# RWKV's key grams, token transpositions and bonuses handed over one piece with every step of the inverse, from the first step on

## The chip, the cores and the metric

The kernel runs on one core of one Trainium2 chip. The metric is the device time of one execution in microseconds (us), as the median of several runs. All matrix work is TensorE's (PE), which multiplies into PSUM banks; VectorE (DVE), ScalarE (ACT) and GpSimd (POOL) move, scale and add; transfers are issued on queues of SP and POOL.

## The reference

A two-layer decoder trunk makes one step for a prompt of 256 tokens and for 8 single sample tokens, 264 columns in all, with a width of 1024, in float32. The part that matters here is the mixer of the even layer, eight heads of stick-breaking attention beside eight heads of RWKV-7:

```python
def rwkv7_recurrence(r, w, k, v, kk, a, s0):
    def step(s, inp):
        r_t, w_t, k_t, v_t, kk_t, a_t = inp
        sa = jnp.einsum('bhij,bhj->bhi', s, kk_t)
        s = (s * w_t[:, :, None, :] - sa[..., None] * (kk_t * a_t)[:, :, None, :]
             + v_t[..., None] * k_t[:, :, None, :])
        return s, jnp.einsum('bhij,bhj->bhi', s, r_t)
...
    y, wkv_final = rwkv7_recurrence(rf, heads(decay), kf, vf, kk, heads(iclr), wkv0.astype(f32))
...
    bonus = jnp.sum(rf * kf * prm['r_k'][i].astype(f32), axis=-1, keepdims=True) * vf
    o_rwkv = ((yn + bonus.reshape(bsz, t, D_RWKV)) * gate).astype(h.dtype)
    out = jnp.concatenate([o_sb, o_rwkv], axis=-1) @ prm['w_out_even'][i]
```

The samples attend to 256 cached keys and values each, gathered from a paged pool.

## The kernel before

Each dense product is done in blocks of 128x128 weights: a weight block is split into a high and a low half (`wh` on ACT, L199; `wl` on DVE, L200), and three matmuls (L297 to L299) use them. The trunk is feed-forward, mixer, feed-forward for each of two layers. The change lies in the even layer's mixer, `_even` (L643), which takes the stretch from about 280 to 417 us.

RWKV's recurrence runs in four chunks of 64 tokens. Before the chain over the chunks (`rwkv_chain`) can start, three things must be there:

- the inverse of a triangular matrix for each chunk and head (`rwkv_inverse`). Its first four steps are the grams of B (L910, into PSUM banks "rk", masked by DVE at L911 into GB). Then come levels 1 to 5, two steps each: `pP` (L935: X times the masked gram `ss`, which DVE makes at L942; ACT copies the result into `st`, L950), and `pX` (L935), after which DVE subtracts it from X (L958) and transposes X into XT (L965). That is 14 steps, and each step waits for the last.
- the pieces of `rwkv_tokens` (L858 on): four grams of K (`GK`, L910 and L911), the transpositions of B and of K to tokens (`tok`, L891, with ACT's copies into BT and KT, L898, two pieces each), four bonuses (`pbn`, L877, and `bon`, L878, which need the values `vr_t`), and the transposition of the values (VT, two pieces): 14 pieces. The K grams, the bonuses and the first half of each transposition use the one PSUM buffer of bank group "sa"; the second half of a transposition uses group "at", with two.
- the input projection's blocks of the values (`pi`, then `pb` on ACT L592, `df` on POOL L595 and L596, `vr_t` on DVE L603). These and the prompt's attention (`z`, `att`, `pcs`, `pov`) come from the generator `other_half`, called `side`.

Two more generators run beside these. `samples` holds the samples' attention: queries are transposed (`pq`, L1166), copied (`qs` on ACT, L1168), written to device memory and spread over partitions (`qd`, `qb`, on POOL's queue, L1170 and L1178), keys are gathered (`kp`, POOL's queue, L1180), multiplied (DVE, L1189) and reduced (DVE, L1190). Later, value pages `vp` are gathered (L1215) and multiplied (`pso`, L1228, in bank "sa"), and DVE masks and reduces the result (L1234, L1236). `states` does the samples' recurrence.

The loop at L685 hands pieces to a scheduler in program order, and that order sets priorities; the scheduler then fixes the order of every engine's queue. With each step of the inverse go two pieces of `side`, and from the fourth step on pieces of `tokens` and `samples` too:

```python
            if i >= 3:
                for _ in range(1 + (i > 8)):
                    next(tokens, None)
                for _ in range((i > 3) + i % 2):
                    next(samples, None)
```

So `tokens` gets one piece at each of steps 3 to 8 and two at each of steps 9 to 13, which is 16 turns; at a turn before stage 2 (the values' projection issued) a bonus that is next takes no piece. What is left is run after the loop, before the chain.

Of the kernel before, what the change touches and what calls it, by code (L numbers as in the profile page):

```python
# [220 lines left out]
class Trunk:  # L221
# [383 lines left out]
    def _even(self, ctx, ln_in, ln_out):  # L605
# [75 lines left out]
        tokens = self.rwkv_tokens(bone)  # L681
# [3 lines left out]
        for i, _ in enumerate(self.rwkv_inverse()):  # L685
            for _ in range(2):
                next(side)
            if i >= 3:
                for _ in range(1 + (i > 8)):
                    next(tokens, None)  # L690
                for _ in range((i > 3) + i % 2):
                    next(samples, None)
        while self.stage < 2:
# [1272 lines left out]
```

## Time and profile before

| what | value |
|---|---|
| runs shown | 1161.09, 1162.82, 1162.86 us; median 1162.82 us |
| profiled execution | 1161.34 us |
| its span | 1159.6 us, mean granted TensorE clock 0.983 |
| PE busy | 1098.3 us (95%) |
| DVE busy | 870.8 us (75%) |
| ACT busy | 592.2 us (51%) |
| POOL busy | 170.4 us (15%) |

Times in the rows are microseconds from the start of the profiled span. A bracket behind a row tells how long the engine had been idle ahead of it and what it then got. "PEclk" is the share of TensorE's full speed that was granted.

### The profile page before, as it was taken

The numbers are of one execution on the slowest core, as the hardware profiler recorded it, in microseconds if no ns is written. First come the engines' busy times: TensorE is split into PE (matmuls) and PEld (weight loads), VectorE is DVE, ScalarE is ACT, GpSimd is POOL, SyncE is SP. The second block draws the span as 40 slices with busy tenths as digits, with TensorE's granted clock in tenths as the row PEclk, the third lists the DMA queues.
The fourth block names the chain that finished last, engine by engine and source line by source line (L and its number), as shares of the span: only waits on it lengthen the run. The fifth ranks groups of instructions, "written<-read, shape, count | busy, mean of one in ns | idle before, by whom it ended". The sixth has DMA issues, their size and how long they took to land. (4 is left out here: it accounts for less than half of the span.)

```text
span 1159.6 us, 25702 instructions
## 1 busy us (share of the span) xinstructions
PE 1098.3 (95%) x10391; PEld 1050.4 (91%) x10391; DVE 870.8 (75%) x1726; ACT 592.2 (51%) x1043; POOL 170.4 (15%) x284
## 2 busy tenths in 40 slices
PE   7999999998889899999999999999969999999996
PEld 7999999987777679999999999999958899999995
DVE  4999855878887969888776888666579689555564
ACT  5544554686344556644454654453363366444442
POOL 0000000355545322011100112000020001000000
PEclk9999999999989999999999999999979999999998
DMA  7654656633455434566775567655474354655551
GB/s 254 231 169 157 211 181 217 199 111 127 155 154 171 150 105 146 169 222 231 256 216 181 163 204 220 204 182 180 146 231 129 117 167 137 210 181 183 181 174 46
DMA packets 66119, 204.91 MB, mean 177 GB/s; under 512 B 13464, under 2 KB 16616, under 8 KB 65744
## 3 DMA queue, kind: packets, MB, share of 16 engines
q1 hardware_dynamic: 56400, 174.09, 47.6%
q0 software_dynamic: 6560, 23.27, 6.1%
q10 hardware_dynamic: 3040, 5.92, 1.6%
q8 instruction: 81, 1.33, 0.5%
q14 instruction: 38, 0.31, 0.1%
HBM read 192.22 MB, written 10.86 MB: 175 GB/s over the span
## 5 line engine op out<-in xcount | busy, mean ns | idle before, releaser
L200 DVE TENSOR_TENSOR wl<-raw,wh 128x1024 fp32r<-128x1024 f32 (+2 forms) x317 | 388.1, 1225 | 183.8 <-ACT wh L199 182.6
L199 ACT CAST wh<-raw 128x1024 fp32r<-128x1024 f32 (+2 forms) x317 | 329.9, 1041 | 320.2 <-issue 103.6
L297 PE MATMUL pd<-hh,wh 128*128 128x264 f32 x704 | 200.8, 285 | 0.0
L299 PE MATMUL pd<-hh,wl 128*128 128x264 f32 x704 | 200.7, 285 | 0.0
L298 PE MATMUL pd<-hl,wh 128*128 128x264 f32 x704 | 199.1, 283 | 0.0
L297 PE MATMUL pg<-xh,wh 128*128 128x264 f32 x648 | 185.0, 285 | 5.6 <-DVE fixc L469 4.0
L299 PE MATMUL pg<-xh,wl 128*128 128x264 f32 x648 | 184.6, 285 | 1.4 <-DVE wl L200 1.3
L298 PE MATMUL pg<-xl,wh 128*128 128x264 f32 x648 | 184.0, 284 | 0.0
L299 PE MATMUL pu<-xh,wl 128*128 128x264 f32 x608 | 172.9, 284 | 1.8 <-DVE wl L200 1.7
L297 PE MATMUL pu<-xh,wh 128*128 128x264 f32 x608 | 172.7, 284 | 0.0
L298 PE MATMUL pu<-xl,wh 128*128 128x264 f32 x608 | 172.3, 283 | 0.0
L297 PEld LDWEIGHTS pd<-hh,wh 128*128 128x128 f32 x704 | 132.4, 188 | 0.6
L299 PEld LDWEIGHTS pd<-hh,wl 128*128 128x128 f32 x704 | 132.6, 188 | 0.2
L298 PEld LDWEIGHTS pd<-hl,wh 128*128 128x128 f32 x704 | 132.4, 188 | 0.0
L297 PEld LDWEIGHTS pg<-xh,wh 128*128 128x128 f32 x648 | 122.6, 189 | 6.5 <-ACT xh L453 4.4
L299 PEld LDWEIGHTS pg<-xh,wl 128*128 128x128 f32 x648 | 122.1, 188 | 2.5 <-DVE wl L200 2.4
L298 PEld LDWEIGHTS pg<-xl,wh 128*128 128x128 f32 x648 | 122.6, 189 | 0.0
L299 PEld LDWEIGHTS pu<-xh,wl 128*128 128x128 f32 x608 | 114.1, 188 | 2.9 <-DVE wl L200 2.9
L297 PEld LDWEIGHTS pu<-xh,wh 128*128 128x128 f32 x608 | 114.8, 189 | 0.0
L298 PEld LDWEIGHTS pu<-xl,wh 128*128 128x128 f32 x608 | 114.8, 189 | 0.0
L500 ACT CAST hh<-h 128x264 fp32r<-128x264 f32 x79 | 32.2, 409 | 55.1 <-DVE h L499 55.1
L297 PE MATMUL raw<-rh,wh 128*128 128x266 f32 x192 | 55.9, 291 | 0.1
(548 smaller groups left out, 2153.6 us busy)
## 6 DMA issues: line engine op xcount, KB each, us to landing
raw<-in_w SPq DMA_DIRECT2D x308, 512.0 KB, 3.7
raw<-in_w SPq DMA_DIRECT2D x7, 384.0 KB, 5.6
gxd<-gc SPq DMA_DIRECT2D x8, 256.0 KB, 3.9
qb<-qd POOLq DMA_DIRECT2D x8, 256.0 KB, 3.3
FT<-wd POOLq DMA_DIRECT2D x8, 256.0 KB, 4.2
bF<-in_bF POOLq DMA_DIRECT2D x8, 256.0 KB
rot<-rotd ACTq DMA_DIRECT2D x5, 384.0 KB, 3.8
rotd<-T POOLq DMA_DIRECT2D x2, 768.0 KB, 6.7
```

Of the source, the lines that this page charges most:

```text
L199: nc.scalar.copy(wh[:, :w], raw[:, :w])
L200: nc.vector.tensor_tensor(out=wl[:, :w], in0=raw[:, :w], in1=wh[:, :w], op=ALU.subtract)
L297: mm(ps, lhsT=wh, rhs=xh, start=start, stop=False)
L298: mm(ps, lhsT=wh, rhs=xl, start=False, stop=False)
L299: self.last_mm = mm(ps, lhsT=wl, rhs=xh, start=False, stop=stop)
L500: self.last = [nc.scalar.copy(hh[:, m, :], h), self.last_mm]
```

## The change

One piece of `tokens` goes with every step from step 0 on, and never two. That is 14 turns. The samples' turns stay as they were.

```diff
         for i, _ in enumerate(self.rwkv_inverse()):
             for _ in range(2):
                 next(side)
+            next(tokens, None)
             if i >= 3:
-                for _ in range(1 + (i > 8)):
-                    next(tokens, None)
                 for _ in range((i > 3) + i % 2):
                     next(samples, None)
```

The set of instructions is the same; their order in the queues differs between about 285 and 417 us. The edit takes one line away, so the changed kernel's line numbers behind it are lower by one. Numbers in names tell versions of a tile apart.

First place: PE's queue between the last grams of B and the first level of the inverse. Before:

```order
L910 MATMUL gram_4012<-ar_3440,K_3441 64x128 x5
L1112 MATMUL pov_4417<-att_3876,vv_3339 64x256
L1112 MATMUL pov_4417<-att_3879,vv_3339 64x256
L1112 MATMUL pov_4417<-att_3876,vv_3339 64x128
L1112 MATMUL pov_4417<-att_3879,vv_3339 64x128
L891 MATMUL tok_4423<-cst_75,B_3442 128x128 x4
L891 MATMUL tok_4503<-cst_75,K_3441 128x128
L1166 MATMUL pq_4022<-cst_75,qk_3338 8x128 x4
L891 MATMUL tok_4503<-cst_75,K_3441 128x128 x3
L910 MATMUL gram_4121<-ar_3440,K_3441 64x128 x8
L935 MATMUL pP_4054<-X_4042,ss_4052 64x64 x16
L935 MATMUL pP_4075<-X_4042,ss_4073 64x64 x16
```

And with the change:

```order
L909 MATMUL gram_4042<-ar_3440,K_3441 64x128 x8
L890 MATMUL tok_4215<-cst_75,B_3442 128x128 x4
L890 MATMUL tok_4369<-cst_75,K_3441 128x128
L934 MATMUL pP_4084<-X_4072,ss_4082 64x64 x9
L1165 MATMUL pq_4052<-cst_75,qk_3338 8x128 x4
L934 MATMUL pP_4084<-X_4072,ss_4082 64x64 x7
L890 MATMUL tok_4369<-cst_75,K_3441 128x128 x3
L890 MATMUL tok_4152<-cst_75,B_3442 128x128 x4
L934 MATMUL pP_4105<-X_4072,ss_4103 64x64 x16
```

All four K grams now stand ahead of `pq` (the first row here is the last of them), each paired with a gram of B; before, one stood there, one followed, and the last two stood ahead of the second level's `pP` and `pX`. `pov` has moved behind the second level, the second piece of B's transposition from behind the second level into the first, and `pq` stands inside the first `pP`.

Second place: DVE's queue ahead of the third level's `pP`, which multiplies by the two `ss` in these rows. Before (the second vr_t and the last K gram's GK stand some rows higher):

```order
L965 STREAM_TRANSPOSE XT_4043<-X_4042 128x512 x2
L1189 TENSOR_TENSOR kp_4199<-kp_4199,qb_4197 128x512
L1189 TENSOR_TENSOR kp_4203<-kp_4203,qb_4197 128x512
L1190 TENSOR_REDUCE sz_4031<-kp_4199 128x8
L1190 TENSOR_REDUCE sz_4031<-kp_4203 128x8
L942 TENSOR_TENSOR ss_4360<-GB0_3890,cst_75 128x512
L942 TENSOR_TENSOR ss_4381<-GB1_3891,cst_75 128x512
L1189 TENSOR_TENSOR kp_4288<-kp_4288,qb_4286 128x512
L878 TENSOR_TENSOR bon_4577<-vr_t_3801,pbn_4581 128x264
```

And with the change:

```order
L1188 TENSOR_TENSOR kp_4228<-kp_4228,qb_4226 128x512
L1188 TENSOR_TENSOR kp_4232<-kp_4232,qb_4226 128x512
L1189 TENSOR_REDUCE sz_4061<-kp_4228 128x8
L1189 TENSOR_REDUCE sz_4061<-kp_4232 128x8
L941 TENSOR_TENSOR ss_4388<-GB0_3890,cst_75 128x512
L941 TENSOR_TENSOR ss_4409<-GB1_3891,cst_75 128x512
L877 TENSOR_TENSOR bon_4451<-vr_t_3801,pbn_4455 128x264
L1188 TENSOR_TENSOR kp_4317<-kp_4317,qb_4315 128x512
```

Only the bonus moves, by one place. Between this vr_t and the first `ss` here stand ten instructions both times: before GK, a reduction, two X, two transposes, two multiplications and two reductions; now a multiplication stands in GK's place. On POOL, the `qb` issue that stood ahead of this vr_t's `df` stands behind it.

Third place: PE's queue at the first step of the chain (`pW`, L983). Before:

```order
L297 MATMUL pi_4817<-xh_3226,wh_4264 128x264
L298 MATMUL pi_4817<-xl_3227,wh_4264 128x264
L299 MATMUL pi_4817<-xh_3226,wl_4265 128x264
L983 MATMUL pW_4835<-VT_4730,GK0_4010 64x64 x4
L983 MATMUL pW_4835<-VT_4730,GK1_4011 64x64 x4
L1032 MATMUL pgt_4844<-gd_3029,g2_3001 128x264
```

And with the change:

```order
L890 MATMUL tok_4821<-cst_75,vr_t_3801 128x128 x4
L982 MATMUL pW_4835<-VT_4730,GK0_3925 64x64 x4
L1031 MATMUL pgt_4844<-gd_3029,g2_3001 128x264
L982 MATMUL pW_4835<-VT_4730,GK1_3926 64x64
L1250 MATMUL psv_4887<-cst_75,sv_3439 48x128
L982 MATMUL pW_4835<-VT_4730,GK1_3926 64x64 x3
```

The second piece of VT's transposition, which stood ahead of the fifth level, now stands directly ahead of `pW`, which reads VT. Further on, at the third chunk's step, `pso`'s first half stands ahead of `pcs` where it stood behind `pgm`, and on DVE L1234 and L1236 stand ahead of the second `att` (L1159).

## Rows read from the trace of the kernel before

**Rows 1.** The page, part 1: busy time of the engines.

```profile
PE 1098.3 (95%) x10391; PEld 1050.4 (91%) x10391; DVE 870.8 (75%) x1726; ACT 592.2 (51%) x1043; POOL 170.4 (15%) x284
```

**Rows 2.** PE's waits, 285 to 420 us: total us, times, longest.

```profile
PE pP L935 <- DVE X L958: 2.7, 2, 2.2
PE pcs L1102 <- DVE att L1159: 2.6, 2, 2.0
PE pso L1228 <- DMA vp<-in_cache_v,idx: 2.1, 2, 1.7
```

**Rows 3.** PE's timeline, levels 2 and 3: start us, us, then idle before.

```profile
307.75 2.08 PE L935 MATMUL pP<-X,ss 64*64 64x64 f32 x64 [2.25 <-DVE X L958]
...
311.42 1.09 PE L910 MATMUL gram<-ar,K 64*64 64x128 f32 x16
312.34 2.09 PE L935 MATMUL pX<-st,XT 64*64 64x64 f32 x64
...
316.60 0.66 PE L891 MATMUL tok<-cst,B 128*128 128x128 f32 x4 [0.52 <-DVE GK L911]
...
318.85 0.66 PE L891 MATMUL tok<-cst,K 128*128 128x128 f32 x4 [1.37 <-ACT BT L898]
321.50 1.25 PE L877 MATMUL pbn<-t,cst 128*128 128x264 f32 x2 [2.00 <-ACT KT L898]
322.68 3.68 PE L935 MATMUL pP<-X,ss 64*64 64x64 f32 x64
```

**Rows 4.** DVE's timeline over the same levels.

```profile
306.00 0.49 DVE L603 SCALAR_TENSOR_TENSOR vr_t<-df,vec,pb 128x264 f32<-128x264 f32 x1 [1.92 <-POOL df L596]
...
310.00 1.27 DVE L1189 TENSOR_TENSOR kp<-kp,qb 128x512 f32<-128x512 f32 x2
...
315.45 0.49 DVE L603 SCALAR_TENSOR_TENSOR vr_t<-df,vec,pb 128x264 f32<-128x264 f32 x1 [1.25 <-POOL df L596]
...
321.82 1.28 DVE L942 TENSOR_TENSOR ss<-GB,cst 128x512 f32<-128x512 f32 x2
```

**Rows 5.** POOL's timeline: the samples' key loads and df.

```profile
296.44 0.63 POOL L1170 DMA_DIRECT2D qd<-qs  x1 [7.54 <-ACT qs L1168]
...
301.13 2.01 POOL L1180 DMA_INDIRECT kp<-in_cache_k,idx  x1 [0.30 <-issue]
...
304.06 0.98 POOL L1180 DMA_INDIRECT kp<-in_cache_k,idx  x1 [0.30 <-issue]
...
310.94 1.21 POOL L1180 DMA_INDIRECT kp<-in_cache_k,idx  x1 [2.81 <-DVE kp L1189]
...
313.88 0.60 POOL L1178 DMA_DIRECT2D qb<-qd  x1
...
315.19 0.23 POOL L596 TENSOR_TENSOR df<-sh_in,pb 128x8 f32<-128x8 f32 x1
```

**Rows 6.** Windows: stretch, length, then each engine's busy time (instructions), PEclk, DMA share, GB/s.

```profile
386.00:407.00 21.00, 18.72 (x211) 12.63 (x209) 20.96 (x37) 11.69 (x29) 5.50 (x7) 1.00 0.35 117
...
321.00:327.00 6.00, 5.50 (x69) 4.71 (x70) 4.93 (x9) 1.83 (x5) 3.57 (x4) 0.50 0.48 152
305.00:308.00 3.00, 0.75 (x18) 0.51 (x16) 2.00 (x4) 0.00 (x0) 2.84 (x8) 1.00 0.81 299
```

**Rows 7.** ACT's copies of VT's second piece, from the timeline.

```profile
344.83 1.49 ACT L898 COPY VT<-tok 64x256 f32<-64x256 f32 x4
```

**Rows 8.** PE's timeline, third chunk of the chain.

```profile
401.23 0.91 PE L1102 MATMUL pcs<-att,cst 128*128 128x384 f32 x2 [1.99 <-DVE att L1159]
...
403.59 1.90 PE L1228 MATMUL pso<-vp,sw 128*32 128x512 f32 x10
...
411.86 1.73 PE L1228 MATMUL pso<-vp,sw 128*32 128x512 f32 x4 [1.74 <-DMA vp<-in_cache_v,idx]
```

**Rows 9.** DVE's timeline, the same chunk.

```profile
402.50 0.68 DVE L1234 TENSOR_TENSOR pv<-pso,cst 128x512 f32<-128x512 f32 x1
...
403.69 1.07 DVE L1236 TENSOR_REDUCE soc<-pv 128x64 f32<-128x512 f32 x1
```

## The prediction

> **What bounds the kernel now.** I read the page's busy shares first. PE is busy 95% of the span, the next engine 75% [rows 1]. So the end moves only if PE has less idle time, or runs less of it at the low clock. The set of instructions doesn't change and only PE's order between about 285 and 417 us does, so I listed PE's waits there [rows 2]: X from DVE 2.7 us, att from DVE 2.6, value pages from a DMA 2.1. The timeline then shows where they lie, and adds some: 2.25 for X, 0.52 for GK, 1.37 for BT, 2.00 for KT [rows 3]. These four make 6.14 us, all within 17 us, and all four are waits that the change touches. Last, the timelines of DVE and POOL show what stands behind those waits [rows 4, 5], and a table of windows gives the clock [rows 6].
>
> **The waits at levels 2 and 3.** The first is X behind vr_t in DVE's queue: vr_t waited until 306.00 for POOL's df, and X came after it [rows 4]. Now X of level 1 stands ahead of vr_t. The K grams moved ahead cost 1.09 each [rows 3], three of them and half a `pP` stand newly ahead of `pq`, `pov` no longer does, so level 1 ends some 1.9 us later. A K gram no longer stands ahead of level 2's `pP`, and nothing waits for X: I put that `pP` at 306.1 instead of 307.75. It is 1.6 us ahead. The K gram of 1.09 ahead of level 2's `pX` is gone too, a `tok` of 0.66 stands there instead, and a half of XT that still stands behind vr_t takes some back; `pX` starts about 310.4 instead of 312.34. The three waits for GK, BT and KT then have nothing to wait for, since those pieces are done a level earlier. With `pX` (2.09), a block of the values' projection (1.6, from the end of level 2's `pP` to the gram at 311.42), `pov` and one bonus behind it, PE reaches level 3's `pP` at about 315.5, where before it started at 322.68 [rows 3].
>
> It can't start there. It needs X of level 2 and its `ss`, which DVE makes at 321.82, after ten instructions behind a vr_t that started at 315.45 and had waited for POOL's df [rows 4]. So from that vr_t to that `ss` DVE was never idle: 6.37 us. The change leaves ten instructions there, one multiplication (half of 1.27) for one GK. So `ss` still comes 6.4 us after vr_t, and the question is when vr_t starts. Its df stands on POOL behind two key loads, and the first of these, at 310.94, had waited for a multiplication of DVE that began at 310.00 [rows 4, 5]. The samples' chain starts at `qd`, 296.44, which waits for `pq` [rows 5]; `pq` ends about 2.7 us later now. Up to 310.94 there were 2.81 us of slack on POOL [rows 5], which takes most of this up: I get the load at 311.35, 0.4 later. Then the `qb` issue of 0.60 ahead of df is gone [rows 5]. Net, vr_t starts 0.2 earlier, `ss` comes a shade earlier still, and `pP` starts at about 322.3 instead of 322.68: **-0.35 us**. The 6.1 us of scattered waits become one of nearly 7 us, for DVE.
>
> The bounds of this term: a key load takes POOL 0.98 to 2.01 us [rows 5]. With the four loads between `qd` and df at the short end, vr_t comes some 1.4 us earlier (but not more, since DVE is busy up to its wait of 1.25 ahead of vr_t); with two of them at the long end, 1.5 later. So -1.8 to +1.2. I take the middle, since the loads keep their neighbours on POOL.
>
> The Trainium skill's "SBUF — State Buffer", section "Who interferes with whom", states that a two-input DVE instruction and a GpSimd instruction that reads SBUF shut each other out of a shared port. By it, df would begin later by up to one such DVE instruction, 0.64 us (half of 1.27 [rows 4]), and the sum would be that much higher; no row here isolates it.
>
> **The clock.** The granted clock is 0.50 from 321 to 327, with 5.50 us of busy time in it; in the window of the 2.25 us wait it stayed at 1.00 [rows 6]. Level 3's `pP` took 3.68 us at that low clock against 2.08 at level 2 [rows 3]. So half of 5.5, some 2.7 us, is lost to the clock there now. I expect the same again after the one long wait: 0.
>
> **VT ahead of `pW`.** The second VT piece leaves its cover. Its `tok` is 0.66 [rows 3], formerly beside a wait for `ss`; ACT's copies take 1.49 [rows 7], and ahead of the matmuls that need them stand only the first half of `pW` and one `pgt`, about 0.7. So +0.6 and +0.9, less what level 3 gave: about **+1.2** at the chain's start, bounds 0 (a filler hides it) and +1.6. But at 401.23 PE waited 1.99 for DVE [rows 8], and DVE was busy 20.96 of the 21 us from 386 [rows 6]. DVE carries its own backlog there, so what PE loses earlier than that (or gains) ends in that wait: I count **0** of both, the -0.35 and the +1.2, as they nearly cancel and the wait is larger than either.
>
> **The third chunk.** `pso`'s first half now stands ahead of `pcs`. It lasts 0.95 (half of 1.90) and can't begin until DVE has read the earlier `pso` at L1234, at about 402.2, so `pcs` comes 1 to 2 us later than 401.23. The value pages that `pso` frees are asked for some 1.4 us sooner, and the last wait there is 1.74 for such a page [rows 8]. On the other side, `att` stands behind L1234 and L1236 on DVE, 0.68 and 1.07 [rows 9]. If the pages decide, -1.4; if PE's own queue does, the 2.1 us of page waits vanish [rows 2] and +1.1 comes for the late `pcs`, -1.0. I take **-0.7**, between ends of -2.1 (both page waits gone, nothing late) and +1.5 (1.75 of DVE work ahead of att, nearly all on PE's path).
>
> **The sum.** 0 + 0 - 0.7 = -0.7 us against the profiled 1161.34, which stands 1.48 below the median of the runs; on the median's scale 1162.82 - 0.7 = **1162.1 us**. A measurement of this kernel can tell about 0.2% (2.3 us) from no change.
>
> **Rivals.**
> - *Faster.* The samples' chain comes early, not late: key loads at the short end, vr_t and `ss` 1.4 earlier. For it: the loads' spread [rows 5], and fewer queued matmuls at level 2. Then -1.8 at level 3 keeps the clock's low stretch shorter too (say a third of 2.7, -0.9), DVE has its backlog 1.4 sooner done, and the page waits go, -1.4. Together -4.1: 1158.7 us. Against: DVE's ten instructions are the same, and `pq` stands later. Chance 0.31.
> - *Slower by the clock.* The one wait of 7 us at level 3, longer than any of the waits listed, drops the clock sooner and keeps it low through the `pX` and the block behind. Another 6 us of busy time at half speed costs up to 3.0, and the -0.35 doesn't make it good. With the +1.2 of VT shown, not swallowed, -0.7 + 3.0 + 1.2 = +3.5 at the most, about +2.9 with half of VT: 1165.7 us. It decides from a low stretch of some 11 us of busy time on. For it: scattered waits brought the clock to 0.50 [rows 6]; against: by that same row the low stretch was as long without a long wait. Chance 0.13. [...]
> - *Slower at the tail.* `pso` ahead of `pcs` with one "sa" buffer: PE stands until L1234, then `att` is 1.75 late and the pages are no sooner. +1.5, and the +1.2 of VT is not swallowed because DVE's backlog ran off earlier: +2.7, 1165.5 us. It decides if PE's wait ahead of `pso` or `pcs` passes 3.5 us (now 1.99). Chance 0.11.
> - The forecast, within 2.3 us of now: 0.45.
>
> **The numbers.** Faster by over 0.2% 0.31, within 0.44, slower 0.25 (the two slower rivals, and a hundredth of the forecast's own upper end). The range of 8 in 10 runs from 1158.6, the faster rival, to 1165.6, the slower ones; the forecast's own bounds (-1.8 - 2.1 and +1.2 + 1.5) lie inside but for the ends. The likeliest case alone: 1160.5 to 1164.5.
>
> **What would show it.** Right: no wait for GK, BT or KT; one wait of 6 to 7 us for DVE ahead of level 3's `pP`, which starts at 322.0 to 322.6; X of level 1 not waited for; a wait for ACT's VT of about 1 us at the first `pW`; `pso` ahead of `pcs` near 402; everything behind 424 shifted by a constant. Wrong: level 3's `pP` before 321 (then it's the faster rival); PEclk of 0.50 beyond 328 or again near 402 (the clock); a wait of over 3.5 us near 402 (the tail).

## The result, and the profile after

The changed kernel takes 1169.6 us (median of 6 runs, 1164.26 to 1171.87) against 1160.7 us for the kernel before, measured beside it: a ratio of 1.0067, with a 95% interval of 1.0053 to 1.0082. It is slower by about 0.7%, or 8 us. (Here and below a ratio is an estimate over all runs of both kernels, with its 95% interval, and not the quotient of the medians, which differ by 8.9 us here.) The ratios leave out two executions that ran far longer than the others of their kernel, 2025.62 us of the kernel before and 1211.98 us of the pacing alone. The forecast was 1162.1 us, no change; the range ended at 1165.6.

The profiled execution of the changed kernel took 1171.87 us. Ahead of the change it already runs 1.2 us late (a matmul of the same name starts at 277.66 instead of 276.45), so times of the two traces are compared less 1.2. PE's waits between 285 and 440 us, in the columns of [rows 2]:

```profile
PE pP L934 <- DVE ss L941: 9.3, 2, 7.5
PE pov L1111 <- ACT att L1104: 6.5, 1, 6.5
PE pso L1227 <- DMA vp<-in_cache_v,idx: 2.7, 3, 1.7
```

The waits for X, GK, BT and KT are gone, and one wait of 7.5 us for `ss` stands in their place: that was forecast. A wait of 6.5 us of `pov` for att was not; in the kernel before `pov` waited 0.29 us at that place. PE's timeline at level 3 and at the third chunk (the first two rows answer to [rows 3]):

```profile
299.77 1.04 PE L1165 MATMUL pq<-cst,qk 128*8 128x128 f32 x8
...
326.54 3.39 PE L934 MATMUL pP<-X,ss 64*64 64x64 f32 x64 [7.52 <-DVE ss L941]
...
378.01 0.68 PE L993 MATMUL pU<-Wn,XT 64*64 64x64 f32 x16
...
395.65 1.11 PE L1111 MATMUL pov<-att,vv 128*64 128x256 f32 x2 [6.52 <-ACT att L1104]
396.69 1.22 PE L1089 MATMUL z<-qk 64*128 64x256 f32 x2
...
402.65 0.68 PE L993 MATMUL pU<-Wn,XT 64*64 64x64 f32 x16
```

Level 3's `pP` starts 2.7 us later than before (326.54 less 1.2, against 322.68). But by the second chunk's `pU` only 0.4 us of that is left: 378.01 less 1.2, against 376.44. By the third chunk's `pU` the lag is 9.6 us: 402.65 less 1.2, against 391.89. So the loss arises between 378 and 403 us. The windows of that stretch, in the columns of [rows 6]:

```profile
388.00:395.00 7.00, 1.13 (x8) 0.73 (x6) 2.85 (x5) 0.00 (x0) 0.89 (x2) 0.95 0.47 156
396.00:401.00 5.00, 5.00 (x39) 2.89 (x37) 2.93 (x6) 1.48 (x5) 0.61 (x1) 0.50 0.29 99
```

PE works 1.13 us in 7, then runs 5 us at a granted clock of 0.50, which costs some 2.5 us more (an estimate: half of the 5). The two make 9.0 of the 9.2 us by which the lag grows. The wait leads back over ACT's att to DVE, and there to one load. POOL's queue and DVE's queue in that stretch:

```profile
377.91 1.09 POOL L1214 DMA_INDIRECT vp<-in_cache_v,idx  x1
379.30 4.49 POOL L1214 DMA_INDIRECT vp<-in_cache_v,idx  x1 [0.30 <-PE pvt L1118]
384.10 0.94 POOL L1214 DMA_INDIRECT vp<-in_cache_v,idx  x1 [0.30 <-issue]
...
387.17 0.60 POOL L1270 DMA_DIRECT2D st<-in_s_wkv_in  x1
```

```profile
378.95 0.68 DVE L1282 TENSOR_TENSOR st<-st,svx 128x512 f32<-128x512 f32 x1
379.55 0.68 DVE L1284 TENSOR_TENSOR ss<-svv,svx 128x512 f32<-128x512 f32 x1
380.15 0.68 DVE L1287 TENSOR_TENSOR ss<-ssa,svx 128x512 f32<-128x512 f32 x1
380.75 0.68 DVE L1285 TENSOR_TENSOR st<-st,ss 128x512 f32<-128x512 f32 x1
381.36 1.01 DVE L1158 SCALAR_TENSOR_TENSOR att<-att 128x384 f32<-128x384 f32 x2
382.29 0.68 DVE L1288 TENSOR_TENSOR st<-st,ss 128x512 f32<-128x512 f32 x1
383.00 0.69 DVE L1290 TENSOR_TENSOR ss<-st,svx 128x512 f32<-128x512 f32 x1
383.62 0.41 DVE L1008 TENSOR_TENSOR S<-S,pS 128x256 f32<-128x256 f32 x1
...
392.15 0.69 DVE L1280 TENSOR_TENSOR ss<-st,svx 128x512 f32<-128x512 f32 x1 [6.68 <-DMA st<-in_s_wkv_in]
...
394.50 1.01 DVE L1103 TENSOR_TENSOR att<-att,pcs 128x384 f32<-128x384 f32 x2
```

One gather of a value page holds POOL's queue for 4.49 us, where its neighbours take about 1 (I call it the held gather). Behind it in the queue, after two more gathers and an addition, stands the load of the samples' third state. DVE waits 6.68 us for that load, until 392.15, and behind the waiting instruction stands the att that ACT and then PE need. While the gather is held, DVE runs additions and multiplications whose two operands both lie in SBUF, one behind the other; the gather ends 0.17 us after DVE starts its first instruction with an operand in PSUM (L1008, 383.62).

In the kernel before, the same gathers took 0.95 to 1.24 us, and the same load was issued at 382.27. Rows of POOL, DVE and PE there:

```profile
381.17 1.10 POOL L1215 DMA_INDIRECT vp<-in_cache_v,idx  x1 [0.16 <-issue]
382.27 0.60 POOL L1271 DMA_DIRECT2D st<-in_s_wkv_in  x1
```

```profile
378.14 0.68 DVE L1283 TENSOR_TENSOR st<-st,svx 128x512 f32<-128x512 f32 x1
379.64 1.79 DVE L1159 SCALAR_TENSOR_TENSOR att<-att 128x384 f32<-128x384 f32 x2 [0.82 <-ACT att L1157]
381.35 0.68 DVE L1286 TENSOR_TENSOR st<-st,ss 128x512 f32<-128x512 f32 x1
381.96 0.68 DVE L1288 TENSOR_TENSOR ss<-ssa,svx 128x512 f32<-128x512 f32 x1
...
385.60 0.69 DVE L1281 TENSOR_TENSOR ss<-st,svx 128x512 f32<-128x512 f32 x1 [1.09 <-DMA st<-in_s_wkv_in]
386.21 0.68 DVE L1292 TENSOR_REDUCE sys<-ss 128x8 f32<-128x512 f32 x1
386.81 0.54 DVE L1104 TENSOR_TENSOR att<-att,pcs 128x384 f32<-128x384 f32 x1
```

```profile
387.96 0.65 PE L1112 MATMUL pov<-att,vv 128*64 128x256 f32 x2 [0.29 <-ACT att L1105]
```

These rows split the delay. `pov` starts 6.5 us later than before (395.65 less 1.2, against 387.96). Of this, 3.7 us is the late issue of the load (387.17 less 1.2, against 382.27), most of it the held gather. Another 1.7 us is the load's way to DVE (5.0 us from issue to the first use, 3.3 before); why it takes longer stays open. The last 1.1 us is DVE's own order: between the load's first use and att now stand `wl` and a state multiplication, where one reduction stood (2.35 us, against 1.21).

On DVE, att stood directly behind the first state write before, and DVE waited 0.82 us for it; one gather, at 378.94, was issued on that gap. In the changed kernel three state instructions stand between that write and att (two of them stood behind att before), so nothing is waited for and there is no gap. The gap alone doesn't explain the difference, though: the gather at 381.17 in the kernel before took 1.10 us beside L1286 and L1288, which have both operands in SBUF and run without a gap.

### The profile page after: what moved, and what is told of

It reads as the page before. It is cut to its first block, busy times and chain, and to the rows that moved or that the text cites. A ratio compares the mean times of both kernels' runs of the same rounds, so it can differ in the third digit from the quotient of the medians.

```text
span 1170.1 us, 25707 instructions
## 1 busy us (share of the span) xinstructions
PE 1100.3 (94%) x10391; PEld 1051.8 (90%) x10391; DVE 870.5 (74%) x1726; ACT 593.0 (51%) x1043; POOL 169.3 (14%) x284
```

## The experiments

The **theory** after the result: the held gather delays the state load, and this alone makes the loss. The **rivals**: level 3's late start, or VT's late piece, carried to the end; or an accident of one execution.

### The changed kernel again

No edit.

> The changed kernel once more, as it is. Theory (queue theory): one value-page gather on GpSimd's queue holds it for 4.5 us instead of 1.0 near 380 us, the third state load queued behind it lands late, and TensorE waits 6.5 us; since this follows from the order of the queues, it should be there again: one gather of over 3 us between 370 and 390, TensorE's wait for ScalarE's att of over 5 us, and a time of 1167 to 1172. Rival (chance): the 4.5 us was an accident of the one profiled execution; then all gathers there take under 2 us and the time is within 3 us of the kernel before plus what level 3 loses, 1163 to 1165.

Measured: 1168.68 us, ratio 1.0063 (1.0042 to 1.0084). Its rows:

```profile
PE pov L1111 <- ACT att L1104: 6.2, 1, 6.2
```

```profile
379.50 4.49 POOL L1214 DMA_INDIRECT vp<-in_cache_v,idx  x1 [0.30 <-PE pvt L1118]
```

The held gather is there again, to the hundredth: it isn't an accident of one execution. Level 3 starts 1.4 us late here (324.40, with 0.36 of offset ahead of the change), against 2.7 in the first execution.

### Twelve memsets on VectorE

```diff
+        gp = self.tw([128, 16], "gp")
+
+        def gap():
+            nc.vector.memset(gp, 0.0)
...
             nc.vector.tensor_tensor(out=S, in0=S, in1=bj(1), op=ALU.mult)
+            gap()
```

(and after the two other writes of S)

> The changed kernel with twelve tiny memsets on VectorE, three in each of the four state steps, each between two multiplications that read two operands from SBUF. They add about 12 x 0.07 us of VectorE work. Queue theory, in the form that the gather is held off as long as VectorE runs instructions with two SBUF operands back to back: the memsets are gaps, no gather takes over 2 us between 370 and 390, the 6.5 us wait for att falls below 2, and the time falls by 4 to 8 us to 1162 to 1166. Rival 1 (the gather is held by the DMA queue's backlog, not by VectorE): the gather still takes over 3 us and the time stays at 1168 to 1171. Rival 2 (the loss is level 3's late start carried to the end): same, 1168 to 1171.

Measured: 1170.74 us, ratio 1.0077 (1.0049 to 1.0104), the gather held for 4.49 us as before. But all twelve memsets ran between 216.1 and 223.4 us, some 150 us ahead of the state steps: nothing in the program depends on them. The run says nothing of the gaps.

### The state loads on SP's queue, in the changed kernel and in the kernel before

```diff
-            nc.gpsimd.dma_start(out=S.rearrange("p i j -> p (i j)"), in_=a["s_wkv_in"][:, 512 * h:512 * h + 512])
+            nc.sync.dma_start(out=S.rearrange("p i j -> p (i j)"), in_=a["s_wkv_in"][:, 512 * h:512 * h + 512])
```

> The changed kernel with the four loads of the samples' states issued from SP's queue instead of GpSimd's. Queue theory: the third load no longer stands behind the gathers, VectorE's wait for it (6.7 us) falls below 3, TensorE's wait for att below 2, and the time falls by 4 to 8 us, to 1162 to 1166, whether or not a gather still takes 4.5 us. Rival (level 3's late start carried to the end): the time stays at 1168 to 1171 even though the load comes earlier.

> Control: the same edit in the kernel before. There VectorE waits 1.1 us for that load and 3.1 for svx, which the edit doesn't touch. Queue theory: within 2 us of the kernel before, 1159 to 1162. If the edit itself gave much (over 3 us faster), the gain of the run before this one would not be the change's.

Measured: the changed kernel with this edit 1160.12 us, ratio 1.0004 to the kernel before (0.9984 to 1.0023); the kernel before with it 1164.53 us, ratio 1.0027 (1.0012 to 1.0043). The changed kernel as it is took 1168.68 beside them. The first run's rows of PE's waits and of POOL:

```profile
PE pP L934 <- DVE ss L941: 9.8, 2, 8.0
...
PE pov L1111 <- ACT att L1104: 0.3, 1, 0.3
```

```profile
376.92 4.47 POOL L1214 DMA_INDIRECT vp<-in_cache_v,idx  x1 [0.30 <-issue]
```

This settles the place of the loss: DVE's wait for that load. The gather is still held (4.47 us), level 3 still waits 8.0 us, VT's second piece still stands directly ahead of `pW`, and only the load no longer stands behind the gather: the wait for att is 0.3 us, and the whole 0.7% is gone. The control shows that it isn't the edit's own merit, since in the kernel before it costs 0.3% (within 2 us had been expected; it is 3).

### Gaps that data keep in place, in the changed kernel and in the kernel before

```diff
+        gp = self.tw([128, 1], "gp")
+
+        def gap(S):
+            nc.vector.tensor_reduce(out=gp, in_=S[:, 0, 0:8], axis=AX.X, op=ALU.add)
...
             nc.vector.tensor_tensor(out=S, in0=S, in1=bj(1), op=ALU.mult)
+            gap(S)
```

(and after the two other writes of S)

> The changed kernel with a tiny VectorE reduction (128x8 to 128x1, one operand) after each of the three writes of a state, whose data keeps it between the multiplications; the memsets of the run before last stood elsewhere in VectorE's queue and told nothing. Lock theory (the gather is held off while VectorE runs instructions with two SBUF operands back to back, and starts at the first gap): the gather that took 4.5 us takes 2.5 or less, the third state load is issued 2 us sooner or more, TensorE's wait for att falls from 6.2 to under 4.5, and the time falls by 2 to 5 us, to 1164 to 1167. Rival (the gather is held by something on its own queue): it still takes 4.4 to 4.6 us and the time stays at 1168 to 1171.

> Control for the kept gaps: the same twelve small reductions in the kernel before, which has no held gather near 380. They cost about 12 x 0.08 us of VectorE. Theory: 1 to 3 us slower than the kernel before (VectorE is busy all through 386 to 407), so that the 0.2% that the changed kernel with gaps stands above before are the gaps' own. Rival: no cost (within 1 us); then some 2 us of the change's loss have another cause than the held gather.

Measured: the changed kernel with gaps 1167.52 us against 1164.05 for the kernel before beside it, ratio 1.0021 (1.0001 to 1.0042), where the changed kernel without gaps had 1.0063 to 1.0067 (measured beside other runs); the kernel before with gaps 1164.1 us against 1162.65, ratio 1.0014 (0.9994 to 1.0034). POOL and DVE in the changed kernel with gaps:

```profile
382.44 1.14 POOL L1214 DMA_INDIRECT vp<-in_cache_v,idx  x1 [0.30 <-issue]
...
387.13 0.60 POOL L1270 DMA_DIRECT2D st<-in_s_wkv_in  x1
```

```profile
382.08 0.68 DVE L1285 TENSOR_TENSOR ss<-st,svx 128x512 f32<-128x512 f32 x1
382.69 0.68 DVE L1290 TENSOR_TENSOR ss<-svv,svx 128x512 f32<-128x512 f32 x1
383.29 0.68 DVE L1286 TENSOR_REDUCE ssa<-ss 128x8 f32<-128x512 f32 x1
...
385.44 0.15 DVE L1276 TENSOR_REDUCE gp<-st 128x1 f32<-128x8 f32 x1
```

The gather that took 4.49 us takes 1.14. The state load is issued 5.2 us after the second chunk's `pU` (381.94), where it was 9.2 (387.17 and 378.01), and the wait for att falls to 1.1 us. That fits the theory of the load.

It doesn't show that the added gaps freed the gather. The first of them stands at 385.44, 1.9 us after the gather had ended. While the gather ran, DVE ran two multiplications and then `ssa`, a reduction that the kernel has anyway and that stood ahead of the held gather in the changed kernel: the edit had shifted the order. Nor does this execution show where the rest of the time goes: it took 1171.3 us, near the longest of its ten, and was already 4.9 us late at the second chunk's `pU`. What is left of the loss in the ratio, 0.2%, is about what the gaps cost by themselves in the control, though the control's interval reaches down to nothing.

### The samples' queries first

```diff
-            if i >= 3:
+            if i == 0:
+                next(samples, None)
+            if i > 3:
                 for _ in range((i > 3) + i % 2):
                     next(samples, None)
```

alone, and together with the state loads on SP's queue:

> The changed kernel with the samples' first turn (pq, qd, the first key loads) given at step 0 instead of step 3. pq then stands among the grams, some 8 us earlier. Theory (level 3 is late only because pq is): TensorE's wait for ss ahead of level 3's pP falls from 8 us to under 4, level 3 starts 3 us or more earlier. On the end: with the queue theory the time is set by whether the gather near 380 is still held; if it is (4.5 us), 1165 to 1170; if not, 1158 to 1161. Rival (level 3's late start is what costs the 8 us): 1160 to 1162 with the 4.5 us gather still there.

> Both edits in the changed kernel: the samples' first turn at step 0, and the state loads on SP's queue. Theory (level 3's late start is taken up by later waits; only the state load behind the held gather costs): level 3's pP starts 3 us or more earlier than with the state loads alone, yet the time is within 2 us of that run. Rival (level 3's late start still costs its 2 to 3 us): 2 to 3 us faster than with the state loads alone, and so faster than the kernel before by 0.2% or more.

Measured: alone 1167.6 us, ratio 1.0033 (1.0004 to 1.0062); with the state loads on SP's queue 1161.33 us, ratio 0.9986 (0.9970 to 1.0003). Alone:

```profile
PE pov L1113 <- ACT att L1106: 3.8, 1, 3.8
PE pP L936 <- DVE ss L943: 3.7, 2, 2.3
PE pP L936 <- DVE X L959: 3.6, 2, 2.3
```

```profile
379.97 4.16 POOL L1216 DMA_INDIRECT vp<-in_cache_v,idx  x1 [0.30 <-PE pvt L1120]
```

With `pq` early, the wait for `ss` ahead of level 3 falls from 7.5 to 2.3 us; the first half of the level's `pP` starts at 318.04 and the second, which had that wait, at 322.91 (326.54 in the changed kernel), while 2.3 us of waiting for X have come back. So level 3 was late because the samples' chain was, which starts with `pq`. The gather is still held, 4.16 us, and the wait for att is still there.

Once the loads are off POOL's queue, the early queries do pay. The run with both edits and the one below, which has only the loads moved, were measured side by side, with twelve executions each: their means are 1161.3 and 1164.1 us, and the difference of 2.7 us has a 95% interval of 1.0 to 4.5 (worked out from the times of the executions). The theory had expected at most 2 us here; so the first rival has a part in it. The edit moves the whole chain of the queries, so not all of the 2.7 need be level 3's. And since the changed kernel with the loads moved stands level with the kernel before, the change must gain about as much elsewhere; that is inferred.

### The state loads on SP's queue once more

> The changed kernel with the state loads on SP's queue once more, beside the others on one chip. Theory: again within 0.25% of the kernel before (0.9985 to 1.0025), with the held gather still there (4.4 to 4.6 us) and no wait of over 1 us for att.

Measured: 1163.77 us, ratio 1.0009 (0.9993 to 1.0024), as expected. One expectation failed: in this profiled execution, the slowest of twelve, no gather was held. Earlier waits, among them one of 2.3 us of PE ahead of `pgm`, had shifted the engines against each other:

```profile
385.81 0.95 POOL L1214 DMA_INDIRECT vp<-in_cache_v,idx  x1 [0.30 <-PE z L1091]
```

```profile
385.26 0.68 DVE L1282 TENSOR_TENSOR st<-st,svx 128x512 f32<-128x512 f32 x1
385.86 0.68 DVE L1284 TENSOR_TENSOR ss<-svv,svx 128x512 f32<-128x512 f32 x1
386.46 0.68 DVE L1287 TENSOR_TENSOR ss<-ssa,svx 128x512 f32<-128x512 f32 x1
387.06 0.72 DVE L1285 TENSOR_TENSOR st<-st,ss 128x512 f32<-128x512 f32 x1
```

This gather runs its 0.95 us beside the first three of the same instructions without being held. So a run of them doesn't hold every gather that falls into it, and what decides stays open.

### Parts of the change alone

The K grams at steps 0 to 3, everything else at its turns of before; and the pacing alone, one piece from step 3 on:

```diff
+            if i < 4:
+                next(tokens, None)
             if i >= 3:
-                for _ in range(1 + (i > 8)):
+                for _ in range((1 + (i > 8)) if i > 6 else 0):
```

```diff
-                for _ in range(1 + (i > 8)):
+                for _ in range(1):
```

> The kernel before with only the four K grams moved to steps 0 to 3; transpositions, bonuses and VT get their turns as before (step 7 on, two from step 9). pq stands behind the grams as in the changed kernel, VT is early as before. If the late pq makes the held gather (svx and the state steps late on VectorE): a gather of over 3 us near 380 and 1166 to 1170. If VT's late piece makes it: no such gather and 1160 to 1163.

> The kernel before with only the pacing changed: one piece from step 3 on, never two. pq and the grams stand as before; bonuses and VT come late, even later than in the changed kernel. If VT ahead of pW makes the loss: a wait for VT at the first pW, a gather of over 3 us near 380, 1165 to 1170. If the late pq makes it: no held gather, and only what VT's wait costs and is not taken up again, 1160 to 1164.

Measured: grams alone 1167.57 us, ratio 1.0027 (1.0012 to 1.0043); pacing alone 1168.71 us, ratio 1.0040 (1.0021 to 1.0059), both beside a kernel before of 1164.05. Neither profile shows a held gather near 380 (1.24 us and less with the grams alone) nor a wait of `pov` for att of over 1.2 us. But the profiled executions are the shortest of the ten of each kernel (1160.03 and 1163.52), so they don't show where the typical one loses. Neither branch of either expectation fits: the times are those of the held gather, the profiles are not. Both parts cost something by themselves, and their two losses add up to that of the whole (0.27 and 0.40%); by which wait each loses stays open.

### The grams and the queries first

The grams at steps 0 to 3 as above, and the samples' first turn at step 0.

> The kernel before with the four K grams at steps 0 to 3 and the samples' first turn at step 0; transpositions, bonuses and VT as before. pq is early and VT is early. Theory: no held gather, no wait for VT at the first pW, less waiting at levels 2 and 3, of which little arrives at the end: within 3 us of the kernel before, likeliest 1 to 2 us faster. If a gather near 380 is held all the same, 4 to 8 us slower.

Measured: 1161.66 us against 1162.65, ratio 0.9982 (0.9966 to 0.9998): 0.2% faster than the kernel before, at the edge of what can be told. No gather near 380 is held. It is the one arrangement whose whole interval lies below the kernel before.

## Why the prediction was wrong

- **The waits for GK, BT, KT and X of level 1** went, as forecast, and one wait for DVE's `ss` took their place: 7.5 and 8.2 us in the two profiled executions of the changed kernel, nearly 7 forecast. The mechanism, `pq` and then vr_t and ten instructions of DVE, was right: from vr_t to `ss` it took 6.4 us in both, as forecast, and early queries shorten the wait to 2.3.
- **Level 3, -0.35 us**: the sign was wrong. It starts 2.7 us late in the first execution and 1.4 in the second, because vr_t does (2.8 and 1.5 us, forecast 0.2 early). `pq`, put 2.7 us later, was 4.1 us later in the first (299.77 less 1.2, against 294.49), of which 1.5 arose among the grams; in the second it was 2.5, about as forecast. What the sum left out is the way of `qd` through device memory behind it:

```profile
298.60 0.59 POOL L1178 DMA_DIRECT2D qb<-qd  x1 [1.53 <-DMA qd<-qs]
```

```profile
301.71 0.63 POOL L1169 DMA_DIRECT2D qd<-qs  x1 [8.79 <-ACT qs L1167]
305.80 0.59 POOL L1177 DMA_DIRECT2D qb<-qd  x1 [3.45 <-DMA qd<-qs]
```

From the issue of `qd` to that of `qb` it took 2.2 us before (the first row, with 296.44 of [rows 5]), 4.1 in the changed kernel (the other two) and 3.8 in its second execution. Together with `pq` that is 6.0 and 4.2 us, more than the 2.81 of slack, and the rest went through to vr_t. The two key loads ahead of df were short in the first execution (0.99 and 0.94) and long in the second (1.45 and 1.97).
- **The clock, 0**: `pP` of level 3 again ran at the low clock (3.39 us, 3.68 before), but the low stretch held less work:

```profile
321.00:327.70 6.70, 6.20 (x72) 5.38 (x72) 5.03 (x9) 1.88 (x5) 3.57 (x4) 0.50 0.49 155
```

```profile
326.50:329.50 3.00, 2.96 (x56) 2.96 (x58) 2.81 (x5) 0.58 (x1) 2.50 (x3) 0.50 0.59 165
```

PE was busy for 6.2 us at 0.50 before (first row) and for 3.0 with the change (4.8 in the second execution), so some 0.7 to 1.6 us less was lost to the clock there (an estimate: half the difference). It fell again behind the wait at the third chunk, 396 to 401, which I had named as a sign of the slower case.
- **VT ahead of `pW`, +1.2**: the size was right. The lag behind the kernel before grows from 1.4 us at the `pvt` ahead of it (353.71 less 1.2, against 351.09) to 2.6 at the first chunk's `pU` (359.71 less 1.2, against 355.91). The sign that I named, a wait for ACT's copies, isn't there: PE fills the time with other matmuls between the pieces of `pW`. Two slips in the sum: 1.49 less 0.7 is 0.8 and not 0.9, and the -0.35 is taken off the +1.2 and then set against it a second time. That earlier losses are taken up again was right: 0.4 us was left at the second chunk's `pU` (1.2 in the second execution). They ended in waits that I had left out (before, `pcs` waited 0.7 us for bon and `pgv` 1.3 for t; both are gone), not, as I wrote, in DVE's wait at 401.
- **"DVE carries its own backlog there"**: this is the step that failed. The sum counts 0 for what comes before the wait at 401, because DVE was busy for 20.96 of the 21 us from 386 on [rows 6]. I took that row as true of the changed kernel too, and gave no term to the stretch from 378 to 400. But the backlog holds only as long as its data are there. In the changed kernel DVE stood idle for 6.68 us, until 392.15, for the third state's load behind the held gather, and att stood behind it. That made 6.5 us of idle PE and about 2.5 at half clock, where the forecast had nothing; with that load on another queue the loss was gone (1.0004 and 1.0009).
- **The third chunk, -0.7**: this can be seen only without that wait. In the changed kernel the lag stayed as it was from the third chunk's `pU` (9.6 us) to the last `pgv` (430.14 less 1.2, against 419.20: 9.7), and the waits for value pages, which were to vanish, were 2.7 us (1.5 in the second execution), against 2.1 before. With the state loads on SP's queue the lag fell by 0.8 over the same stretch, close to the forecast. `pso` stood ahead of `pcs`, as I had said.
- **The rivals**: "slower at the tail" had the sign and nearly the place, but neither the mechanism (`pso`, the "sa" buffer) nor the size, +2.7 for 8. None of them has a late state load. I had read the spread of the key loads, 0.98 to 2.01 us [rows 5], as a bound of one term; whether it has to do with the held gather isn't shown. Of six held gathers near 380, in six profiled executions, each ended 0.17 to 0.18 us after DVE's first instruction with an operand in PSUM.

The Trainium skill's "SBUF — State Buffer", section "Who interferes with whom", states that a two-input DVE instruction and a GpSimd instruction that reads SBUF exclude each other, whole instruction against whole instruction. I had cited it for df, with a price of one DVE instruction, 0.64 us. Whether it is what held the gather, no run isolates. The held gather's 4.49 us would fit it if the gather found no place between seven instructions that DVE started one behind the other. But the unheld gathers, at 381.17 in the kernel before and at 385.81 in the repetition with the state loads on SP's queue, ran beside such instructions too. What a gather needs to slip in between two of them was not tried.

## What to carry to other kernels

When a reorder moves only a few rows of a queue, walk every in-order queue of the whole stretch that differs, not only the places where the large blocks moved: a load behind a slow issue, behind it an engine, behind that engine another one, cost here 8 us. A transfer that something waits for should not stand in a queue behind transfers whose issue can take 1 us or 4.5: one changed queue name took back the whole loss here, though it cost 0.3% in the kernel before, which had no such gather. And a wait that is removed is worth only the distance to the next thing that is late, so find first what gates the step after it.

## What the runs showed of the hardware

- The issue of one indirect gather on GpSimd took 4.16 to 4.49 us in six profiled executions, and 0.95 to 1.24 for those near it in the kernel before. In the changed kernel the DMA engines' share was 0.00 from 382 to 384 us, with the gather still held. Why it is held in one execution and not in another stays open.
- In the kernel before, VectorE's att pair took 1.79 us beside a GpSimd addition (379.90 to 381.01). In the changed kernel it took 1.01 us, with the held gather beside it and no addition. This is one pair; it isn't shown that the addition was the reason.
- An instruction that no data tie to its place can run far from where the program writes it: the twelve memsets ran some 150 us early. A gap that is meant to stay has to be part of a chain of data.
